# Down-projection sums issued at a wider spacing, and four raw buffers for the seven-product weight loads

## Chip, cores and metric

The kernel runs on one core of one Trainium2 chip. The metric is device time in microseconds for one execution of the whole program. Three runs of the kernel before are given, and one further execution was profiled.

## What is computed

Two layers (DEPTH = 2) of a hybrid encoder on a sequence of 512 tokens, width 1024, in float32. In short:

```python
for l in range(DEPTH):
    h = _rmsnorm(x, g_mix[l])
    proj = h @ w_in[l]            # gates (4 x 1024), conv input, q/k/v of three attentions
    y_a = _conformer_conv(...)    # branch 0
    y_b = _neighbourhood_attn(...)  # branch 1
    y_c = _dilated_attn(...)      # branch 2
    y_d = _window_gqa_sink(...)   # branch 3
    branch = jnp.einsum('bsnc,ncd->bsnd', ys, w_branch[l])
    gates = jax.nn.sigmoid(gate_pre + gate_b[l])
    x = x + jnp.sum(gates * branch, axis=2) @ w_out[l]
    x = x + _conv_ffn(_rmsnorm(x, g_ffn[l]), w_up[l], ffn_conv_w[l], ffn_conv_b[l], w_down[l])
```

`_conv_ffn` multiplies by `w_up` (1024 x 5632), applies a width-3 depthwise convolution, SwiGLU, and multiplies by `w_down` (2816 x 1024).

## The kernel before

All products are made from split operands: a float32 value is a rounded part `hi` plus a remainder `lo`, and each product is three matmuls (`hi*hi`, `hi*lo`, `lo*hi`). Activations lie with channels on the partitions (eight tiles of 128 x 512). Weights come in units of 128 x 1024 floats, 512 KB each. The method `weights` loads a unit: a DMA on SP's queue into a buffer `raw`, an ACT copy that rounds it to `hi` (line 252), and a DVE subtraction that gives `lo` (line 254). There are three `hi`, three `lo` and, for most units, two `raw` buffers (`w_raw`). A list `w_list` holds the units in order, each with a number in front. Units of the down-projection have the number 0, and for those a counter `w_fast` sends two of every four to two further buffers, `w_more`, that live in the pool of the feed-forward stage.

A layer runs in this order: token-major projections of q, k and v, the conformer branch's gated input (`glu`), then for the branches in the order 1, 2, 3, 0 the eight gate blocks of each branch (`gates`), the output projection, and the feed-forward stage. A block is 24 matmuls on one unit. In `gates`, each of the eight columns `d` ends with an elementwise chain: DVE multiplies the gate and the branch product into `t` (line 878), POOL adds it to the running sum `mx` (line 879; DVE does so for the last two columns of the last gate), and in the last gate ACT and DVE then split the sum into `mh` and `ml` (lines 883 and 884).

Beside the blocks run generators in `self.side`: attention, the convolution, and the transfers of sums described next. They advance by one step at each `tick`, which the code calls once in the middle of a block and once behind it. When the third gate is done, the line

```python
while self.side:
    self.tick()
```

runs what is left of them to the end, before the last gate (branch 0) is emitted.

The two large matrices of the feed-forward stage are multiplied in blocks of two by two with seven products instead of eight (a Strassen-Winograd form). That needs sums of weight blocks, S1 to S4, and these are formed by DMA: transfers from HBM to HBM on POOL's queue, some of which add into their destination. `quarter_sums` makes the sums for the up-projection (five groups of eight transfers, 512 KB each, line 1110), and `weight_sums` those for the down-projection (line 1133): four sums in three chunks, 1024, 1024 and 768 KB, 24 transfers. Each transfer is "paced": it may be issued only after the matmul that was emitted last. They are chained in one generator in `layer`:

```python
self.side.append(self.slowly(chain(self.quarter_sums(l), self.weight_sums(l))))
```

`slowly` waits 12 ticks, and then as many ticks after each transfer as the generator yields (one where it yields nothing). The order in `weight_sums` is: three copies into s3, three into s1, three additions into s3, three into s1, three copies of s3 into s2, three additions into s2, three copies of s2 into s4, three additions into s4. An operation on a chunk waits for the earlier one on which it depends.

In the feed-forward stage the up-projection runs over eleven groups of channels. Groups 2 to 6 use the seven-product form: `seven` takes one unit for each of the products, 24 matmuls of 256 columns on each (line 992). The units of A11, A22 and A12 come from the packed weights `W`, those of S1 to S4 from the sums (`qS` in the trace). The other groups are whole blocks. The down-projection follows (`down`), with units from `W` and from `sums`.

The order of instructions on each engine's queue is settled by a planner when the program is built, from priorities and its own times; weight loads are given a priority 3000 instructions ahead of their place.

Of the kernel before, what the change touches and what calls it, by code (L numbers as in the profile page):

```python
# [218 lines left out]
class Trunk:  # L219
# [7 lines left out]
    def weights(self, upto, ahead=3000, parts=1, queue=None):  # L227

        nc = self.nc
        while self.w_emitted < min(upto, len(self.w_list)):  # L230
            n, pieces = self.w_list[self.w_emitted]
            with self.tc.high_priority(offset=ahead):

                self.w_fast = (self.w_fast + 1) % 4 if n == 0 else 0
                if n == 0 and self.w_fast in (3, 0):
                    raw = self.fp.tile([P, 1024], F32, name="w_raw", tag="w_more", bufs=2)
                else:
                    raw = self.wpool.tile([P, 1024], F32, name="w_raw", tag="w_raw", bufs=2)
                hi = self.wpool.tile([P, 1024], F32R, name="w_hi", tag="w_hi", bufs=3)
                lo = self.wpool.tile([P, 1024], F32R, name="w_lo", tag="w_lo", bufs=3)  # L240
                src = pieces()
                n = sum(p.shape[1] for p in src)
                if len(src) == 1:
                    cut = [slice(i * n // parts, (i + 1) * n // parts) for i in range(parts)]
                    src = [src[0][:, s] for s in cut]
                c = 0
                for p in src:
                    (queue or nc.sync).dma_start(raw[:, c:c + p.shape[1]], p)
                    c += p.shape[1]
                for i in range(parts):  # L250
                    s = slice(i * n // parts, (i + 1) * n // parts)
                    w = nc.scalar.activation(hi[:, s], raw[:, s], AF.Copy)  # L252
                    self.first_hi = self.first_hi or w
                    nc.vector.tensor_tensor(lo[:, s], raw[:, s], hi[:, s].bitcast(F32), ALU.subtract)  # L254
            self.w_ready.append((hi, lo))
            self.w_emitted += 1
# [874 lines left out]
    def weight_sums(self, l):  # L1131

        add = lambda *a, **k: self.paced(self.nc.gpsimd.dma_start(*a, **k))
        items = []
        for c in range(0, NP2, CHUNK):
            n = min(CHUNK, NP2 - c)
            t = self.dram.tile([n * P, 4 * S], F32, name=f"sums{c}", tag=f"sums{c}", bufs=2)
            self.sums[l].append(t)
            src = self.all_quads[l][c * P:(c + n) * P]
            part = lambda x, i: x[:, i * S:(i + 1) * S]  # L1140
            items.append((part, t, src))
        s2, s1, s3, s4 = range(4)
        b11, b12, b21, b22 = range(4)
        for d, s in ((s3, b12), (s1, b11)):
            for part, t, src in items:
                add(part(t, d), part(src, s))
                yield 2
        for d, s in ((s3, b11), (s1, b21)):
            for part, t, src in items:
                add(part(t, d), part(src, s), accum_op=ALU.add)  # L1150
                yield 2
        for d, b, s in ((s2, s3, b21), (s4, s2, b22)):
            for part, t, src in items:
                add(part(t, d), part(t, b))
                yield 2
            for part, t, src in items:
                add(part(t, d), part(src, s), accum_op=ALU.add)
                yield 2

    def pair_tags(self, j):  # L1160

# [161 lines left out]
    def run(self):  # L1323
        nc, tc = self.nc, self.tc
        with ExitStack() as st:
            pool = lambda name, **k: st.enter_context(tc.tile_pool(name=name, bufs=1, **k))
            self.const = pool("const")
            self.xpool = pool("xparts")
            self.wpool = pool("weights")
            self.norm = pool("norm")  # L1330
            self.psum = pool("psum", space=PSUM)
            self.dram = pool("dram", space=bass.MemoryType.DRAM)
            self.w_list = []
            self.quads, self.sums, self.all_quads, self.quarters, self.qsums = [], [], [], [], []
            self.halves = {}
            for l in range(L):
                off, quads, quarters, ups, sums = 0, [], {}, {}, {}
                for kind, a, n in UNITS:
                    src = self.W[l, off:off + n * P].rearrange("(p c) -> p c", p=P)
                    off += n * P  # L1340
                    if kind == 'quad':
                        quads.append(src)
                    elif kind == 'quarter':
                        quarters[a] = src
                    elif kind == 'up':
                        ups[a] = src
                    else:
                        self.w_list.append((n, lambda src=src: [src]))
                for kind, a, b in UP_STEPS:
                    if kind == 'whole':  # L1350
                        self.w_list.append((1024, lambda src=ups[b * DFF + a * P]: [src]))
                    elif b[0] == 'A':
                        self.w_list.append((1024, lambda src=quarters[a, int(b[1]) - 1, int(b[2]) - 1]: [src]))
                    else:
                        self.w_list.append((1024, lambda s=sums, at=(a, b): [s[at]]))
                self.quarters.append(quarters)
                self.qsums.append(sums)
                self.quads.append(quads)
                self.sums.append([])
                self.all_quads.append(self.W[l, off - NP2 * 2048 * P:off].rearrange("(p c) -> p c", c=2048))  # L1360
                self.last_units(l)
            self.w_emitted = self.w_used = 0
            self.first_hi = None
            self.w_ready, self.w_fast = [], 0
            self.side, self.waiting, self.head = [], [], None

            self.cst = self.const.tile([P, NRES], F32, name="cst", tag="cst", bufs=1)
            self.ident = self.cst[:, C_ID:C_ID + P]
            self.prm = self.const.tile([P, NPAR], F32, name="prm", tag="prm", bufs=1)
            warm = self.const.tile([P, 1], F32, name="warm", tag="warm", bufs=1)  # L1370
            with tc.tile_pool(name="first", bufs=1, reuse_waits="tile") as first:

                z = first.tile([P, 256], F32R, name="zero", tag="zero", bufs=1)
                nc.vector.memset(z.bitcast(F32), 0.0)
                nc.vector.memset(warm, 0.0)
                ps = self.aux()
                for i in range(WARM):
                    nc.tensor.matmul(ps[:, :256], lhsT=z[:, :P], rhs=z, start=True, stop=True)
                self.sq_tag = "sq"
                self.start_norm('g_mix')  # L1380
                x0 = first.tile([P, KT + S], F32, name="x0", tag="x0", bufs=1)
                self.gains = lambda d: x0[:, d:d + 1]
                for d in range(KT):
                    if d == 0:
                        xn = x0[:, KT:]
                        for s in (slice(0, KT + 256), slice(KT + 256, KT + S)):
                            nc.sync.dma_start(x0[:, s], self.X0[:, s])
                    else:
                        xn = first.tile([P, S], F32, name="xn", tag="xn", bufs=7)
                        nc.sync.dma_start(xn, self.xT[d - 1])  # L1390
                    if d == 0:
                        self.weights(1, 0, 2, nc.scalar)
                        nc.scalar.activation(warm, warm, AF.Exp)
                    self.norm_tile(d, xn, first, d == 0)
                    if d in (1, 3):
                        self.weights(2 + d // 2, 0)
                    if d == 2:
                        nc.sync.dma_start(self.prm, self.PAR[0])
                nc.sync.dma_start(self.cst, self.CST[:, :NRES])
                self.finish_norm(7, 10)  # L1400
            self.xres = [self.X0[:, KT:]] + [self.xT[d] for d in range(KT - 1)]
            for l in range(L):
                self.layer(l)
# [124 lines left out]
```

## Time and profile before

| | |
|---|---|
| runs | 1597.1, 1598.54, 1599.13 us |
| median | 1598.54 us |
| profiled execution | 1600.03 us, of which its span 1598.3 us |
| mean granted TensorE clock | 0.991 |
| busy in the span | PE 97%, DVE 78%, ACT 56%, POOL 13% |
| DMA queue of SP | 212.10 MB, 41.6% of 16 engines |
| DMA queue of POOL | 92.81 MB, 26.0% of 16 engines |

PE is TensorE's matmuls, PEld its weight loads, DVE VectorE, ACT ScalarE, POOL GpSimd, SP the engine that issues most DMAs. A "q" behind an engine's name is its queue (SPq). Shares are of the span. A row of the timeline gives the start in us, the duration, the engine, the line of the kernel, the operation and its tiles, and in brackets how long the engine had been idle and what ended that; "x2" marks neighbours that are merged. Rows of DMA issues show the issue and not the transfer. Row labels such as `sums<-W` read "written from".

### The profile page before, as it was taken

The numbers are of one execution on the slowest core, as the hardware profiler recorded it, in microseconds if no ns is written. First come the engines' busy times: TensorE is split into PE (matmuls) and PEld (weight loads), VectorE is DVE, ScalarE is ACT, GpSimd is POOL, SyncE is SP. The second block draws the span as 40 slices with busy tenths as digits, with TensorE's granted clock in tenths as the row PEclk, the third lists the DMA queues.
The fourth block names the chain that finished last, engine by engine and source line by source line (L and its number), as shares of the span: only waits on it lengthen the run. The fifth ranks groups of instructions, "written<-read, shape, count | busy, mean of one in ns | idle before, by whom it ended". The sixth has DMA issues, their size and how long they took to land.

```text
span 1598.3 us, 21942 instructions
## 1 busy us (share of the span) xinstructions
PE 1547.3 (97%) x7842; PEld 1312.7 (82%) x7842; DVE 1252.9 (78%) x2114; ACT 895.3 (56%) x1504; POOL 204.3 (13%) x308
## 2 busy tenths in 40 slices
PE   9999999996999999999999999999969999899999
PEld 8888888884889988888888878888858898888887
DVE  6699988752689989895676989887446888899964
ACT  6778777332456655563557677763234555554642
POOL 0044112332100000000002231132221000000000
PEclk9999999998999999999999999999989999999999
DMA  7789786999654543366567978769986466633565
GB/s 234 225 226 244 190 204 191 214 230 231 202 177 132 175 160 128 93 202 203 178 195 224 242 208 198 197 186 234 245 204 222 158 166 187 185 122 104 174 215 172
DMA packets 124797, 306.84 MB, mean 192 GB/s; under 512 B 28176, under 2 KB 30096, under 8 KB 124688
## 3 DMA queue, kind: packets, MB, share of 16 engines
q1 hardware_dynamic: 93712, 212.10, 41.6%
q0 software_dynamic: 30688, 92.81, 26.0%
q8 instruction: 62, 1.02, 0.3%
q10 hardware_dynamic: 288, 0.52, 0.1%
q14 instruction: 47, 0.39, 0.1%
HBM read 287.56 MB, written 100.67 MB: 243 GB/s over the span
## 4 chain that ended last, share of the span: by engine, by line
PE 73%; DMA 10%; DVE 9%; ACT 5%; issue 2%; POOL 1%; ACTq 0%; DVEq 0%; POOLq 0%
PE mm L273 14%; PE mm L275 14%; PE mm L274 14%; PE aux L992 4%; DVE w_lo L254 3%; DMA w_raw<-W 3%; DMA w_raw<-qS 3%; DMA sums<-W 3%; PE aux L1224 2%; PE aux L1223 2%; PE aux L1225 2%; ACT w_hi L252 2%; PE mm L1224 2%; PE mm L1223 2%; PE mm L1225 2%
## 5 line engine op out<-in xcount | busy, mean ns | idle before, releaser
L252 ACT ACTIVATE w_hi<-w_raw 128x1024 fp32r<-128x1024 f32 (+1 forms) x335 | 350.6, 1047 | 360.9 <-PE mm L274 127.9
L254 DVE TENSOR_TENSOR w_lo<-w_raw,w_hi 128x1024 fp32r<-128x1024 f32 (+1 forms) x335 | 406.3, 1215 | 110.3 <-ACT w_hi L252 108.6
L273 PE MATMUL mm<-xh,w_hi 128*128 128x512 f32 x960 | 377.0, 393 | 28.1 <-DVE t L849 27.1
L275 PE MATMUL mm<-xh,w_lo 128*128 128x512 f32 x960 | 375.8, 391 | 0.0
L274 PE MATMUL mm<-xl,w_hi 128*128 128x512 f32 x960 | 375.4, 391 | 0.0
L273 PEld LDWEIGHTS mm<-xh,w_hi 128*128 128x128 f32 x960 | 181.2, 189 | 65.9 <-ACT w_hi L252 27.9
L275 PEld LDWEIGHTS mm<-xh,w_lo 128*128 128x128 f32 x960 | 180.8, 188 | 39.5 <-DVE w_lo L254 1.4
L274 PEld LDWEIGHTS mm<-xl,w_hi 128*128 128x128 f32 x960 | 181.3, 189 | 36.2
L992 PE MATMUL aux<-form,w_hi 128*128 128x256 f32 x640 | 117.2, 284 | 1.3 <-ACT w_hi L252 1.1
L992 PEld LDWEIGHTS aux<-form,w_hi 128*128 128x128 f32 x640 | 99.8, 192 | 2.3 <-ACT w_hi L252 2.1
L440 DVE SCALAR_TENSOR_TENSOR cv<-cv,prm 128x512 f32<-128x512 f32 x120 | 94.0, 783 | 0.7
L992 PE MATMUL aux<-form,w_lo 128*128 128x256 f32 x320 | 91.0, 285 | 2.5 <-DVE w_lo L254 2.5
L1033 ACT ACTIVATE cy<-U,prm 128x512 f32<-128x512 f32 x88 | 69.9, 806 | 26.2 <-DVE U L1017 14.3
L879 POOL TENSOR_TENSOR mx<-mx,t 128x512 f32<-128x512 f32 x44 | 63.1, 1440 | 133.6 <-DVE t L878 133.5
L502 PE MATMUL mm<-w_hi,xh 128*128 128x512 f32 x192 | 76.4, 398 | 0.4 <-DVE V L630 0.4
L503 PE MATMUL mm<-w_lo,xh 128*128 128x512 f32 x192 | 75.0, 390 | 0.0
L504 PE MATMUL mm<-w_hi,xl 128*128 128x512 f32 x192 | 74.8, 390 | 0.0
L1110 POOL DMA_DIRECT2D qS<-W x60 | 43.7, 728 | 218.0 <-PE aux L780 107.2
L767 ACT ACTIVATE e<-e,rl 128x256 f32<-128x256 f32 (+2 forms) x96 | 57.4, 598 | 22.0 <-DVE rl L766 21.5
L1034 DVE SCALAR_TENSOR_TENSOR cy<-U,prm,cy 128x512 f32<-128x512 f32 x88 | 64.7, 745 | 6.2 <-ACT cy L1033 6.2
L849 DVE TENSOR_TENSOR t<-mm,RB 128x512 f32<-128x512 f32 x64 | 43.8, 685 | 29.3 <-PE mm L275 29.2
L1035 DVE SCALAR_TENSOR_TENSOR cy<-U,prm,cy 128x512 f32<-128x512 f32 x88 | 64.8, 745 | 0.8
(339 smaller groups left out, 3193.0 us busy)
## 6 DMA issues: line engine op xcount, KB each, us to landing
w_raw<-W SPq DMA_DIRECT2D x213, 512.0 KB, 3.7
qS<-W POOLq DMA_DIRECT2D x60, 512.0 KB, 6.4
sums<-W POOLq DMA_DIRECT2D x24, 1024.0 KB, 13.7
w_raw<-qS SPq DMA_DIRECT2D x40, 512.0 KB, 3.5
w_raw<-W SPq DMA_DIRECT2D x66, 256.0 KB, 3.9
w_raw<-sums SPq DMA_DIRECT2D x44, 256.0 KB, 4.0
w_raw<-sums SPq DMA_DIRECT2D x22, 512.0 KB, 4.6
qS<-qS POOLq DMA_DIRECT2D x20, 512.0 KB, 4.8
```

The lines of the kernel that those rows point to most:

```text
L252: w = nc.scalar.activation(hi[:, s], raw[:, s], AF.Copy)
L254: nc.vector.tensor_tensor(lo[:, s], raw[:, s], hi[:, s].bitcast(F32), ALU.subtract)
L273: mm(ps, lhsT=wh, rhs=xh, start=start, stop=False)
L274: mm(ps, lhsT=wh, rhs=xl, start=False, stop=False)
L275: self.last_mm = mm(ps, lhsT=wl, rhs=xh, start=False, stop=stop)
L440: self.after_mm(v.scalar_tensor_tensor(acc, u[:, t:t + S], w(t), acc, ALU.mult, ALU.add))
L502: mm(pss[b], lhsT=self.Xh[k][:, t], rhs=hi[:, s], start=k == 0, stop=False)
L503: mm(pss[b], lhsT=self.Xh[k][:, t], rhs=lo[:, s], start=False, stop=False)
L504: self.last_mm = mm(pss[b], lhsT=self.Xl[k][:, t], rhs=hi[:, s], start=False, stop=k == KT - 1)
L992: self.last_mm = nc.tensor.matmul(o, lhsT=w[:, s], rhs=x, start=start and not (e or j or i), stop=j == 3 and i == 2, skip_group_check=True)
L1033: nc.scalar.activation(y, u[:, 1:513], AF.Identity, scale=w(1), bias=self.par('ffn_conv_b', c))
L1035: v.scalar_tensor_tensor(y, u[:, 2:514], w(2), y, ALU.mult, ALU.add)
```

## The change

There are two edits. In `weight_sums`, each `yield 2` becomes `yield 4`: a down sum for every four ticks (half blocks) instead of two. In the list of units, those of the seven-product groups get the number 1 instead of 1024, and `weights` lets units with that number take `w_more` and `w_raw` by turns, so that they go through four raw buffers instead of two. The count by which the down-projection's units choose their buffers is not altered, since whole units stand before them and set `w_fast` to 0.

```diff
-                self.w_fast = (self.w_fast + 1) % 4 if n == 0 else 0
-                if n == 0 and self.w_fast in (3, 0):
+                self.w_fast = (self.w_fast + 1) % 4 if n < 2 else 0
+                if n == 0 and self.w_fast in (3, 0) or n == 1 and self.w_fast % 2 == 1:
                     raw = self.fp.tile([P, 1024], F32, name="w_raw", tag="w_more", bufs=2)
                 else:
                     raw = self.wpool.tile([P, 1024], F32, name="w_raw", tag="w_raw", bufs=2)
...
         for d, s in ((s3, b12), (s1, b11)):
             for part, t, src in items:
                 add(part(t, d), part(src, s))
-                yield 2
+                yield 4
...
# the same in the other three loops of weight_sums
...
                     elif b[0] == 'A':
-                        self.w_list.append((1024, lambda src=quarters[a, int(b[1]) - 1, int(b[2]) - 1]: [src]))
+                        self.w_list.append((1, lambda src=quarters[a, int(b[1]) - 1, int(b[2]) - 1]: [src]))
                     else:
-                        self.w_list.append((1024, lambda s=sums, at=(a, b): [s[at]]))
+                        self.w_list.append((1, lambda s=sums, at=(a, b): [s[at]]))
```

More of the change, by code (lines that the diff above doesn't have):

```diff
@@ L1150, in weight_sums @@
                 add(part(t, d), part(src, s), accum_op=ALU.add)
-                yield 2
+                yield 4
         for d, b, s in ((s2, s3, b21), (s4, s2, b22)):
@@ L1154, in weight_sums @@
                 add(part(t, d), part(t, b))
-                yield 2
+                yield 4
             for part, t, src in items:
                 add(part(t, d), part(src, s), accum_op=ALU.add)
-                yield 2
+                yield 4
     def pair_tags(self, j):
```

## The prediction

> **What bounds the kernel now.** I read the head of the page first, then the waits, then the timeline of POOL around the one place where PE stands still, then busy time by stretches.
>
> ```profile
> span 1598.3 us, 21942 instructions
> PE 1547.3 (97%) x7842; PEld 1312.7 (82%) x7842; DVE 1252.9 (78%) x2114; ACT 895.3 (56%) x1504; POOL 204.3 (13%) x308
> ```
>
> PE is busy 1547.3 of 1598.3 us: TensorE is the bound, and only 51.0 us of the span are not matmul. Whatever the change does to the time, it does by shortening or lengthening those 51.0 us. The waits say where the largest pieces lie.
>
> ```profile
> ACT mh L883 <- POOL mx L879: 67.4, 10, 23.7
> DVE ml L884 <- ACT mh L883: 60.1, 10, 23.2
> PE mm L273 <- DVE t L849: 27.1, 2, 14.9
> ```
>
> Columns: who waited for whom, total us, times, longest. PE waits twice (once in each layer) for the DVE product `t` of line 849, 27.1 us in all. The two rows above it say why DVE is late: `ml` waits for ACT's `mh`, which waits up to 23.7 us for POOL's addition `mx` (line 879). So in each layer POOL holds up ACT, DVE and then PE. What POOL does at that time, in layer 0 (start, us, engine, line, operation, and in brackets its idle time and what ended it):
>
> ```profile
> 227.76 0.66 POOL L1133 DMA_DIRECT2D sums<-W  x1 [2.71 <-PE aux L780]
> 236.24 0.65 POOL L1133 DMA_DIRECT2D sums<-W  x1 [7.82 <-PE aux L780]
> ...
> 322.38 0.67 POOL L1133 DMA_DIRECT2D sums<-sums  x1 [5.86 <-PE aux L478]
> ...
> 333.24 0.64 POOL L1133 DMA_DIRECT2D sums<-sums  x1
> ...
> 340.16 0.59 POOL L1133 DMA_DIRECT2D sums<-sums  x1
> 340.77 1.68 POOL L879 TENSOR_TENSOR mx<-mx,t 128x512 f32<-128x512 f32 x1
> 342.39 2.12 POOL L1133 DMA_DIRECT2D sums<-W  x2
> 347.02 0.95 POOL L1133 DMA_DIRECT2D sums<-W  x1 [2.51 <-DMA sums<-sums]
> 358.24 0.66 POOL L1133 DMA_DIRECT2D sums<-sums  x1 [10.26 <-DMA sums<-W]
> 365.40 0.65 POOL L1133 DMA_DIRECT2D sums<-sums  x1 [6.51 <-DMA sums<-W]
> 369.72 0.59 POOL L1133 DMA_DIRECT2D sums<-sums  x1 [3.67 <-DMA sums<-W]
> 373.03 1.04 POOL L1133 DMA_DIRECT2D sums<-W  x1 [2.72 <-DMA sums<-sums]
> 376.27 1.04 POOL L1133 DMA_DIRECT2D sums<-W  x1 [2.20 <-DMA sums<-sums]
> 378.41 0.95 POOL L1133 DMA_DIRECT2D sums<-W  x1 [1.09 <-DMA sums<-sums]
> 379.02 1.63 POOL L879 TENSOR_TENSOR mx<-mx,t 128x512 f32<-128x512 f32 x1
> ```
>
> There are 24 down-sum transfers in a layer. Fourteen are issued one by one from 227.76 to 333.24. From 340.16 on, ten are issued in a row, each as soon as the transfer that it reads from has landed, and the first `mx` addition of the last gate stands behind all ten, at 379.02. In between PE uses up its four banks and stops. This is the place the first edit touches.
>
> **Why ten, and how many after it.** The two generators that transfer sums advance by one step at each tick, and a tick comes twice in a block. From the place where they are started to the end of the third gate the code ticks 80 times: 8 in each of the three `token_major` projections, 8 in `glu`, 16 in each of three `gates`. Before: 12 ticks of waiting, 40 quarter sums at one each, leaves 28 ticks; at two each that is 14 down sums. The rest, 10, is issued by `while self.side: self.tick()`, a loop with no matmul in it, so that pacing by the last matmul no longer holds anything apart. The rows agree: the 15th issue is the one at 340.16. After: 28 ticks at four each are 7 down sums, and 17 go through the loop. The wider spacing thus applies to seven transfers and takes the spacing from seven more. In order these seven are numbers 8 to 14: two additions into s3, three into s1, and two copies s3 to s2, that is 5 accumulating transfers and 2 copies.
>
> **Price of a transfer.** Windows of layer 0 (busy us of each engine with counts, granted clock, DMA share, GB/s):
>
> ```profile
> 227.00:282.00 55.00, 55.00 (x270) 46.20 (x269) 47.28 (x97) 40.89 (x103) 15.30 (x14) 1.00 0.63 191
> 282.00:310.00 28.00, 28.00 (x126) 23.12 (x126) 20.02 (x27) 8.55 (x13) 8.04 (x8) 1.00 1.04 218
> 310.00:343.00 33.00, 33.00 (x155) 27.41 (x154) 24.79 (x46) 14.03 (x18) 11.39 (x11) 1.00 0.92 235
> 343.00:368.00 25.00, 24.83 (x110) 20.24 (x108) 5.56 (x6) 3.90 (x5) 3.77 (x5) 1.00 1.06 239
> 368.00:383.00 15.00, 0.22 (x1) 0.25 (x2) 1.66 (x3) 1.91 (x3) 4.92 (x5) 0.64 1.05 242
> 460.00:495.00 35.00, 35.00 (x156) 29.00 (x155) 35.00 (x56) 20.65 (x26) 0.00 (x0) 1.00 0.34 112
> ```
>
> The last row has whole up-projection blocks and no sums: weight loads alone take 0.34 of the DMA engines while PE runs. From 227 to 282 six copies are issued; they account for (0.63 - 0.34) x 55 = 16 us, or 2.7 us each. From 282 to 343 six additions and a little over two copies: (1.04 - 0.34) x 28 + (0.92 - 0.34) x 33 = 38.7 us; less 2.3 x 2.7, by six, 5.4 us for an addition (it reads its destination too). From 343 to 383 the share is 1.06 and 1.05: in the loop the DMA engines are full, and the issues come at the rate at which transfers finish. Check on the loop as it is: 7 transfers must land before the 24th can be issued, three additions and four copies, 16.2 + 10.8 = 27.0 us, and loads for the 27 us for which PE still runs, 9.2 us: 36.2. Layer 0 took 378.41 - 340.16 = 38.3 us, and layer 1:
>
> ```profile
> 1133.29 0.59 POOL L1133 DMA_DIRECT2D sums<-sums  x1
> ...
> 1169.02 0.94 POOL L1133 DMA_DIRECT2D sums<-W  x1 [0.72 <-DMA sums<-sums]
> ```
>
> 35.7 us, on average 37.0, or 1.02 times the price.
>
> **First edit, the sum.** Removed from the gates: seven transfers a layer. It saves nothing there, since PE is busy 55.00 of 55, 28.00 of 28 and 33.00 of 33 us in those stretches; DMA time that was hidden by matmuls is what is given up. Added to the loop: 5 x 5.4 + 2 x 2.7 = 32.4 us, by 1.02, 33 us a layer. None of it is hidden: PE stops after the same blocks as now, since it is DVE that stands at `ml` and the banks that run out, and no weight load is added while it stands. So PE's standstill grows from about 15 to about 48 us in layer 0 and from 12 to 45 in layer 1: +66 us. Behind the first `mx` on POOL stand the next additions, and behind them the residual loads of the up-projection; they shift as a whole. The first load that reads the sums is issued ahead, on SP:
>
> ```profile
> 454.35 0.86 SPq L248 DMA_DIRECT2D w_raw<-sums  x2
> ```
>
> that is 75 us after the last issue of sums, and both shift alike, so their landing keeps its cover. Bounds: the seven move 4,608 + 2,048 KB, 6.82 MB; at the 242 GB/s of the row 368 to 383 that is 28 us a layer (+56). If each of the seven costs what the loop's seven cost on average, 38.3/7 and 35.7/7 us, it is +74. If all the loop's time but the copies belonged to its three additions, (38.3 - 10.8)/3 = 9.2 us each, it would be 5 x 9.2 + 5.4 = 51 a layer, +103. I take 33, since the prices by share reproduce the loop to 2%; the issue instructions are 0.6 to 1.1 us each and vanish in the waits.
>
> **Second edit.** No instruction is added or taken away: the same loads go into four buffers in turn. What limits the seven-product stage now (layer 1, chain and windows):
>
> ```profile
> 1338.66 1.14 DVE w_lo L254
> 1339.82 4.35 DMA w_raw<-qS
> 1344.28 1.07 ACT w_hi L252
> 1345.37 1.24 DVE w_lo L254
> 500.00:540.00 40.00, 40.00 (x335) 40.00 (x334) 37.27 (x52) 25.19 (x33) 0.00 (x0) 1.00 0.54 175
> 540.00:600.00 60.00, 56.59 (x452) 54.92 (x451) 53.72 (x70) 36.13 (x47) 0.00 (x0) 1.00 0.52 166
> 1290.00:1410.00 120.00, 109.33 (x845) 104.38 (x844) 105.72 (x139) 67.96 (x90) 0.00 (x0) 1.00 0.63 181
> ```
>
> A load may start only when the DVE subtraction has freed its buffer; load, ACT copy and subtraction then take 1346.6 - 1339.8 = 6.8 us, for two buffers 3.4 us a unit, while a unit of 24 matmuls of 256 columns takes 40/335 x 24 = 2.9 us of PE. With four buffers that ring is 1.7 us a unit and no longer binds. PE's idle time there is 3.4 + 10.7 = 14.1 us, the most there is to gain. What comes next is DVE: it is busy 53.72 of 60 and 105.72 of 120 us, and where PE had no gap (500 to 540) it reached 37.27 of 40, 93%. At 93% the two stretches take 57.8 and 113.7 us: 2.2 + 6.3, I take 8 us. Ends: 0 (DVE is late anyway) and 14.
>
> **Sum.** The profiled execution took 1600.0 us, a span of 1598.3 and 1.7 around it; the median of the runs is 1598.5, 1.5 lower, and I add to that. 1598.5 + 66 - 8 = 1656.5, so 1656 us.
>
> **Rivals.** (A) The order on POOL's queue is settled when the program is built, by a planner that goes by its own times. With a longer loop it may put the first `mx` of the last gate ahead of the last few issues. It interleaves like that in the gates (340.77 stands between two issues), but in the loop it left all ten ahead, seven of them waiting. Each column let through gives PE about one interval of the later additions,
>
> ```profile
> 384.51 1.28 POOL L879 TENSOR_TENSOR mx<-mx,t 128x512 f32<-128x512 f32 x1 [3.86 <-DVE t L878]
> 389.64 1.28 POOL L879 TENSOR_TENSOR mx<-mx,t 128x512 f32<-128x512 f32 x1 [3.86 <-DVE t L878]
> ```
>
> 5.1 us: one a layer, 1656 - 10 = 1646. (B) Transfers that follow each other without a pause run faster than these prices: at a copy's 2.7 us for all seven, 18.9 a layer, 1598.5 + 38 - 8 = 1628. Against it: the share is already 1.05 in the loop. The Trainium skill, "DMA: Bandwidth & Descriptors", section Bandwidth, has transfers gain with size, up to 425 GB/s for 16 MB; by that the extra 6.82 MB would take an estimated 16 us a layer and the time would be 1623. That section measures loads from HBM into SBUF; the rows here, HBM to HBM with additions, show 242 GB/s at a full share, so the trace does not agree. (C) Additions are dearer, 9.2 us, because full engines slow them: 1598.5 + 103 - 8 = 1693. For it: the issue at 358.24 waited 10.26 us for the first; against it, the next two follow after 7.2 and 4.3. (D) The other side: the planner puts the last gate's `mx` additions ahead of every issue that has to wait. Then the 27.1 us of standstill go as well, 1598.5 - 27 - 8 = 1563. It decides from the point at which at least seven of the 17 stand behind the first `mx`, since then no more stand ahead than the ten now. Against it: the ten rows above.
>
> **How the numbers follow.** My forecast, 17 transfers ahead of the first `mx` at these prices, has 0.66, and its own range is 1640 to 1674 (from 28 us a layer with the full 14 gained, to +74 with nothing gained, rounded). A 0.15, B 0.05, C 0.09, D 0.05. The range 1632 to 1680 takes in A with cheap transfers and half of what lies between my forecast and C; outside are B, D and most of C, under 0.2. A difference of 0.2%, 3.2 us, is about what a measurement can tell from none; only D can be faster (0.04) or the same (0.01), the rest, 0.95, is slower.
>
> **What would show it.** Right: seven down-sum issues from about 228 to 325 us, then 17 in a row from about 340; the first `mx` after them near 412 instead of 379; PE still from about 367 to 415 with a DMA share near 1; the wait of PE on DVE's `t` near 93 us instead of 27.1; the same in layer 1. In 1290 to 1410 (shifted) PE idle of 4 to 6 us instead of 10.7, with ACT's wait for loads from the quarter sums mostly gone and DVE above 0.9. Wrong: `mx` rows of the last gate between the issues (A, D), issue spacings under 3 us (B) or above 8 for additions (C), or PE idle unchanged in the seven-product stage.

## The result, and the profile after

The changed kernel takes 1638.9 us (median, 1637.9 to 1641.2) against 1598.8 us before on the same chip: a ratio of 1.0254, 95% interval 1.0236 to 1.0272. It is 40.1 us slower. The prediction said 1656, with 1632 to 1680 as its range.

The head of the page and the waits (who waited for whom, total us, times, longest us) after the change:

```profile
span 1637.4 us, 21918 instructions
PE 1541.0 (94%) x7842; PEld 1311.0 (80%) x7842; DVE 1251.0 (76%) x2114; ACT 895.8 (55%) x1504; POOL 205.4 (13%) x308
...
PE mm L273 <- DVE t L849: 89.5, 2, 45.1
ACT mh L883 <- POOL mx L879: 130.9, 10, 55.7
DVE ml L884 <- ACT mh L883: 123.8, 11, 55.2
```

The three waits of before are the same three, with the same count on PE: two standstills, now 89.5 us together instead of 27.1. Below is what POOL did in layer 0, as a timeline:

```profile
337.36 1.02 POOL L1133 DMA_DIRECT2D sums<-W  x1
338.04 1.65 POOL L879 TENSOR_TENSOR mx<-mx,t 128x512 f32<-128x512 f32 x1
339.27 3.41 POOL L1133 DMA_DIRECT2D sums<-W  x3
351.42 0.95 POOL L1133 DMA_DIRECT2D sums<-W  x1 [8.74 <-issue]
356.62 1.32 POOL L1133 DMA_DIRECT2D sums<-sums  x2 [4.25 <-issue]
365.55 0.59 POOL L1133 DMA_DIRECT2D sums<-sums  x1 [7.61 <-issue]
377.85 1.05 POOL L1133 DMA_DIRECT2D sums<-W  x1 [11.70 <-DMA sums<-sums]
...
408.15 0.95 POOL L1133 DMA_DIRECT2D sums<-W  x1 [1.25 <-DMA sums<-sums]
408.76 1.62 POOL L879 TENSOR_TENSOR mx<-mx,t 128x512 f32<-128x512 f32 x1
```

Seven issues stand in the gates (not shown, 227.35 to 322.08); the eighth is the one at 337.36, the first of the 17 that follow each other to 408.15. The first addition of the last gate is at 408.76, where the prediction had 412. The loop took 70.8 us here and 70.1 in layer 1, against 38.3 and 35.7 before. PE stands still from 367 until this:

```profile
412.52 0.76 PE L273 MATMUL mm<-xh,w_hi 128*128 128x512 f32 x1 [45.10 <-DVE t L849]
```

The seven-product stage went the other way. Windows over it, the changed kernel first and the one before below it (busy us with counts, granted clock, DMA share, GB/s):

```profile
525.00:623.30 98.30, 98.30 (x819) 98.18 (x819) 93.35 (x122) 64.71 (x85) 0.00 (x0) 1.00 0.55 178
1340.00:1438.00 98.00, 98.00 (x816) 97.88 (x815) 94.07 (x122) 63.61 (x82) 0.00 (x0) 1.00 0.74 205
```

```profile
495.00:598.00 103.00, 99.59 (x817) 98.18 (x816) 93.75 (x122) 63.88 (x83) 0.00 (x0) 1.00 0.51 163
1286.00:1399.00 113.00, 102.33 (x817) 98.88 (x816) 99.16 (x130) 64.12 (x84) 0.00 (x0) 1.00 0.64 183
```

The same number of matmuls, 816 or a few more, takes 98.0 us after and 103.0 and 113.0 before. After the change a matmul follows each 0.12 us with no gap.

Stage times from the starts of matmuls in the two traces, in us:

| from, to | before | after | difference |
|---|---|---|---|
| last gate, branch matmuls, layer 0 | 54.23 | 85.03 | +30.8 |
| the same, layer 1 | 52.06 | 84.83 | +32.8 |
| 34 seven-product units, layer 0 | 102.99 | 97.79 | -5.2 |
| the same to the next stage, layer 1 | 203.08 | 187.88 | -15.2 |
| end of layer 0's down-projection to the first branch of layer 1 | 160.61 | 156.95 | -3.7 |
| everything else | | | -0.4 |

(The fourth row runs on to the start of the down-projection.) The sum is 39.1 us, the difference of the two spans.

### The profile page after: what moved, and what is told of

The parts are those of the page before. It is cut to its first block, busy times and chain, and to the rows that moved or that the text cites. A ratio compares the mean times of both kernels' runs of the same rounds, so it can differ in the third digit from the quotient of the medians.

```text
span 1637.4 us, 21918 instructions
## 1 busy us (share of the span) xinstructions
PE 1541.0 (94%) x7842; PEld 1311.0 (80%) x7842; DVE 1251.0 (76%) x2114; ACT 895.8 (55%) x1504; POOL 205.4 (13%) x308
## 4 chain that ended last, share of the span: by engine, by line
PE 83%; DMA 6%; DVE 4%; ACT 3%; issue 3%; POOL 2%; SPq 0%; POOLq 0%; ACTq 0%; DVEq 0%
PE mm L273 15%; PE mm L274 15%; PE mm L275 15%; PE aux L992 11%; DMA sums<-sums 4%; PE aux L1225 2%; PE aux L1223 2%; PE aux L1224 2%; PE mm L502 2%; PE mm L504 2%; PE mm L503 2%; PE mm L1224 2%; PE mm L1225 2%; PE mm L1223 2%; PE mm L992 2%
## 5 line engine op out<-in xcount | busy, mean ns | idle before, releaser
L273 PE MATMUL mm<-xh,w_hi 128*128 128x512 f32 x960 | 377.3, 393 | 89.5 <-DVE t L849 89.5
L884 DVE SCALAR_TENSOR_TENSOR ml<-mx,mh 128x512 fp32r<-128x512 f32 x16 | 11.0, 690 | 124.0 <-ACT mh L883 123.8
L883 ACT ACTIVATE mh<-mx 128x512 fp32r<-128x512 f32 x16 | 10.0, 627 | 135.4 <-POOL mx L879 130.9
```

The lines of the kernel that those rows point to most:

```text
L273: mm(ps, lhsT=wh, rhs=xh, start=start, stop=False)
```

## Experiments

Each of the first three kernels below differs from one of the two in one thing. Theory Q, mine: POOL works its queue in order, the issues of sums in the loop wait there for earlier transfers, and the additions that the last gate needs stand behind them; the number of transfers in the loop sets the time. Rival D: it is the DMA traffic itself that costs, wherever the additions stand.

**The two edits apart.** First edit alone: the four `yield 4` in the kernel before. Second alone: `yield 2` put back in the changed kernel.

> The first edit alone (a down sum for every four ticks, two raw buffers as before). Theory Q: the time of the loop that issues what is left of the sums sets how long PE stands still, and the second edit acts elsewhere. Then this run has the standstills of the changed kernel, 45.1 + 44.4 = 89.5 us against 27.1, and the seven-product stages of before: 1598.8 + 62 + 1 = 1662 us. Rival R: a part of the gain in the seven-product stages comes from the first edit (sums out of the way earlier or later, loads that come otherwise): then the units of layer 1 take clearly less than the 112.8 us of before, and the time is 1640 to 1655. The start of layer 1 up to the first sum took 228.0 us before and 224.4 after; 224.4 here would put that to the first edit.

> The second edit alone (four raw buffers, a sum for every two ticks). Theory Q: the standstills are those of before, 27.1 us together, and the 34 units between the first and the last but one of a layer take 97.8 us in each layer (no gap at all) instead of 103.0 and 112.8: 1598.8 - 20.2 = 1578 us, or 1575 if the 3.6 us at the start of layer 1 go with this edit. My prediction's value for this edit, 8 us with DVE as the next limit, gives 1591; the 14.1 us of PE idle that the profile counts give 1585.

Measured: the first edit alone 1661.1 us (ratio to before 1.0408, 1.0372 to 1.0444), the second alone 1576.0 us (0.9869, 0.9842 to 0.9896). The stages are as independent as theory Q has them. With the first edit alone the 34 units take 103.7 and 113.8 us as before, and PE stands still 86.3 us. With the second alone they take 97.8 us twice, and PE stands still 23.6 us. The waits of each (first edit, then second):

```profile
PE mm L273 <- DVE t L849: 86.3, 2, 44.0
```

```profile
PE mm L273 <- DVE t L849: 23.6, 2, 14.1
```

Rival R falls. The start of layer 1 took 228.1 us with the first alone and 227.7 with the second alone, against 224.4 with both, so the 3.7 us of the table belong to neither edit alone.

**The additions off POOL's queue.** In the changed kernel:

```diff
-        (v if n == ORDER[3] and d >= 6 else nc.gpsimd).tensor_tensor(m, m, t, ALU.add)
+        (v if n == ORDER[3] else nc.gpsimd).tensor_tensor(m, m, t, ALU.add)
```

> The changed kernel, with all eight mx additions of the last gate on DVE (before: the first six on POOL). The 17 transfers stay where they are on POOL's queue, but nothing that PE needs stands behind them. Theory Q (the queue): the standstill goes, PE waits for DVE's t under 10 us in all, six DVE additions of 0.7 us a layer lie beside matmuls: 1638.9 - 89.5 + 0 to 8 = 1550 to 1558 us. Rival D (full DMA engines): it is the transfers themselves that hold up the last gate by delaying weight loads, wherever the additions stand; then the 70 us of 17 transfers at a share near 1 still cost half or more of the standstill, 1590 us or more, with PE waiting for ACT's w_hi, and that for loads.

Measured: 1575.0 us (0.9868, 0.984 to 0.9895), midway between the two. The last gate's branch matmuls take 37.40 us in both layers, and the wait of PE for DVE's `t` is gone from the list: the standstill was POOL's queue, as theory Q says. But 26 us of the 89.5 come back behind it (30 by the stage times: the two last gates became 95 us shorter, since behind a standstill about ten matmuls also start some 0.43 us apart, at a granted clock of 0.50 from 412.5 to 415.5 in the changed kernel, and later ones 0.23). From the end of the output projection to the first seven-product matmul it takes 54.9 and 55.9 us instead of 44.65, and the output projection 47.7 and 46.7 instead of 42.84. Windows of this kernel, and a stretch of its chain of waits (start, us, what):

```profile
370.00:400.00 30.00, 27.32 (x120) 22.08 (x119) 18.47 (x25) 10.23 (x14) 3.70 (x4) 1.00 1.05 276
400.00:415.00 15.00, 15.00 (x61) 12.22 (x60) 6.36 (x8) 4.87 (x7) 2.28 (x3) 0.89 1.04 327
415.00:460.00 45.00, 39.62 (x155) 30.01 (x154) 24.43 (x36) 19.16 (x27) 6.53 (x14) 0.92 1.01 303
```

```profile
376.61 8.08 DMA w_raw<-W
384.80 1.07 ACT w_hi L252
385.89 1.24 DVE w_lo L254
387.14 8.47 DMA w_raw<-W
...
427.58 11.96 DMA w_raw<-W
```

With PE at work the full DMA engines (share 1.01 to 1.05) carry loads and sums together, and a weight load takes 8 to 12 us; it took 3.8 in the median of the whole execution of the changed kernel. The residual's stores `res` and loads `xf`, on which the way to the seven-product stage depends, slow down as well: 6.3 us against 2.8 and 8.9 against 3.9, medians of the two executions. So the cost that rival D names is there, but it is a third of the standstill and not the half or more that rival D had. In the changed kernel it did not show: there the output projection and the way behind it take the 42.84 and 44.65 us of before, and PE was standing while the sums went through.

**Additions or copies.** The changed kernel with `accum_op=ALU.add` left out everywhere in `weight_sums`, so that the sums are not formed; only its times are used.

> The changed kernel with every additive transfer of the down sums turned into a plain copy of the same size and place in the queue (so the sums are not formed). In the loop 14 transfers must land before the last issue. By the prices of the prediction (5.4 us an addition, 2.7 a copy, loads of 0.34 for 27 us) it goes from 70.5 to 14 x 2.7 + 9.2 = 47 us, the standstills from 89.5 to about 43, the time from 1638.9 to about 1592. Rival: additions and copies cost the same in a full queue, because bytes or issues limit it: the loop stays at 65 to 71 us and the time above 1625.

Measured: 1604.0 us, one run. The loop takes 50.6 and 51.1 us instead of 70.8 and 70.1, the standstills 49.6:

```profile
338.82 0.63 POOL L1133 DMA_DIRECT2D sums<-W  x1
...
389.43 0.59 POOL L1133 DMA_DIRECT2D sums<-W  x1 [1.23 <-DMA sums<-sums]
390.03 1.27 POOL L879 TENSOR_TENSOR mx<-mx,t 128x512 f32<-128x512 f32 x1
```

Of the 14 transfers that must land before the last issue eight were additions; turning them into copies saved 20.2 us in layer 0 and 19.0 in layer 1, 2.5 and 2.4 us each, near the 2.7 of the prices (5.4 less 2.7). The rival, equal cost, falls. The loop takes 50.6 us and not 47 although a copy costs what the prices say, since the DMA engines are not full in it:

```profile
339.00:390.00 51.00, 29.88 (x132) 24.40 (x130) 7.31 (x8) 5.10 (x6) 11.82 (x18) 0.82 0.94 320
```

0.94 x 50.6 is 47.6 us of their time, less 9.2 for loads, by 14, 2.7 us a copy. That makes the standstills 6.6 us longer than the 43 expected. The rest of the 12 us between 1592 and 1604 lies outside the loop: 2.5 us at the start of layer 1 and 1.4 before the first gate, against the changed kernel.

**Carrying the sums on.** Two kernels in which the loop stops when only the sums are left, one at four ticks and one at two (the second edit in both):

```diff
-                self.side.append(self.slowly(chain(self.quarter_sums(l), self.weight_sums(l))))
+                slow = self.slowly(chain(self.quarter_sums(l), self.weight_sums(l)))
+                self.side.append(slow)
...
-                while self.side:
+                while any(g is not slow for g in self.side):
```

> The changed kernel, but the loop behind the third gate no longer runs the sums to the end: it stops when only the generator of the sums is left, and the remaining 17 transfers go on at one for every four ticks through the last gate and the up-projection. Theory Q: the loop is the cause of the standstill, both by the queue and by the full DMA engines, and with the transfers apart neither remains: 1638.9 - 89.5 = 1549 us, PE waiting for DVE's t under 5 us. Rival D: the sums cost their DMA time wherever they run; most of them now fall into the seven-product stage, whose loads already take a DMA share of 0.55 to 0.74, and 13 transfers of about 5 us each in it bring back 10 us or more of waits for loads: 1560 us or more.

> The second edit alone (one transfer for every two ticks) with the same carrying on past the third gate: ten transfers are left, and eight of them fall into the last gate. Theory Q: the 24.4 us of standstill of the second edit alone go: 1576 - 24 = 1552 us. Against the kernel that carries on at four ticks, the difference shows what the wider spacing is worth when the loop is out of the way: if transfers two ticks apart hold up the mx additions of the last gate (issues that wait for the transfer before them, a DMA share of 1.04 as from 282 to 310), 5 to 15 us, 1557 to 1567; if not, the two are equal within 3 us.

Measured: 1583.8 us (0.9926, 0.991 to 0.9943) at four ticks, 1571.8 us (0.9848, 0.9833 to 0.9863) at two. The last gate takes 37.40 us in both, with no loop no standstill. Both miss the 1549 and 1552 of theory Q, for two reasons. At four ticks the sums are still running in the seven-product stage, whose 34 units take 112.5 us in layer 1 instead of 97.8, at a DMA share of 0.96 there (second row; the first is layer 0):

```profile
489.00:588.00 99.00, 98.29 (x817) 98.02 (x816) 92.82 (x121) 64.59 (x84) 7.99 (x9) 1.00 0.90 263
1269.00:1381.00 112.00, 99.86 (x813) 98.85 (x812) 93.71 (x121) 62.51 (x81) 7.98 (x9) 0.97 0.96 254
```

That is rival D's cost, 14.7 us. In layer 0 nine sums run beside the stage as well and cost 1.0 us (98.8 us). Without sums the share is 0.55 there and 0.74 in layer 1 (the windows after the change), so that layer 1 has less room; that this is the whole reason is not shown. And in both kernels the way from the output projection to the first seven-product matmul takes 55.7 to 58.3 us. POOL in the kernel with two ticks:

```profile
437.26 1.05 POOL L1133 DMA_DIRECT2D sums<-W  x1 [46.52 <-DVE xl L336]
...
438.05 4.25 POOL L943 DMA_DIRECT2D xf<-res  x7
451.07 0.54 POOL L943 DMA_DIRECT2D xf<-res  x1 [8.77 <-DMA sums<-W]
```

One sum stands 46.5 us on POOL: by the code it is paced by a matmul in the first block behind the output projection, and the profile names DVE's `xl`, which that block reads, as what ended the wait. The residual loads `xf` that the seven-product forms are made of stand behind it; seven go out at once at 438. With no sum in front (the second edit alone) they go out one by one from 421. Two ticks came out 12 us faster than four, where the expectation had them equal or two ticks slower: the seven-product stage, which that expectation did not price, costs 15.7 us more at four ticks. The same queue, a second time, with loads behind the waiting issue instead of additions. To test that, the loads went to SP:

```diff
-                nc.gpsimd.dma_start(x[:, e * S:(e + 1) * S], self.xres[2 * j + e])
+                nc.sync.dma_start(x[:, e * S:(e + 1) * S], self.xres[2 * j + e])
```

> The kernel that carries the sums on past the third gate at two ticks, with one difference: the eight residual loads xf, with which the seven-product forms are made, go out on SP's queue and not on POOL's. In that kernel the last gate had no standstill (37.4 us), but from the end of the output projection to the first seven-product matmul it took 55.9 and 58.3 us instead of 44.65, with seven xf loads issued at once at 438 behind a sum that had waited 46.5 us. Theory Q: that loss is POOL's queue once more; with the loads on SP it takes 44.65 us again and the time is 1571.8 - 24.9 = 1547 to 1550 us. Rival: it is the sums' DMA traffic; then the loads land no earlier, and the time stays at 1565 us or more. A third way: the loads stand behind waiting weight loads on SP instead and come late there, 1555 to 1565.

Measured: 1562.5 us (0.9788, 0.9767 to 0.9808), the third way. The stretch falls to 52.9 and 53.4 us, not to 44.65. The first loads still go out only at 437.71, now behind the weight loads on SP:

```profile
437.19 0.42 SPq L248 DMA_DIRECT2D w_raw<-W  x1
437.71 1.03 SPq L943 DMA_DIRECT2D xf<-res  x2
441.96 0.33 SPq L248 DMA_DIRECT2D w_raw<-W  x1
442.33 2.44 SPq L943 DMA_DIRECT2D xf<-res  x5
```

So moving them took 8.0 us off the two stretches together and put them behind another queue. That POOL's queue alone made the whole loss is not shown; that the forms wait for loads that leave late is (waits of the kernel with two ticks, 434 to 492, and the same kernel with the loads on SP, 425 to 485):

```profile
ACT xf L950 <- DMA xf<-res: 10.8, 1, 10.8
```

```profile
ACT xf L950 <- DMA xf<-res: 13.3, 6, 4.6
```

**Fewer in the loop, additions on DVE.** With 26 us left to the full engines, a loop of ten instead of 17 should lose less.

> All additions of the last gate on DVE, as in the run before, but with the spacing of two ticks, so ten transfers in the loop. With 17 in the loop 1575.0 us were left where 1549 would be with no standstill: 26 us for loads that took 8 us instead of 3.7 beside full DMA engines. If that loss goes with the time for which the engines are full (38 of 71 us), it is 14 us here: 1563 us. If it is set by something else (the residual loads and the first up-projection units behind the loop), it stays near 26: 1575 us. If it goes away, 1550 us.

Measured: 1550.9 us (0.9718, 0.9703 to 0.9732). The last gate takes 37.40 us, the output projection 44.4 and 45.9, and the way to the seven-product stage is back at 44.65. The loss is 4.6 us, not the 14 of a loss in proportion. With ten in the loop the last issue stands before the output projection, which begins at 390.6; with 17 it was at 418.96, and the output projection began at 391.9:

```profile
377.42 0.95 POOL L1133 DMA_DIRECT2D sums<-W  x1 [0.64 <-DMA sums<-sums]
```

So most of the stretch in which loads were late at 17 is spared. This version beats both kernels.

**The other spacings.**

> Four raw buffers, and a sum for every tick: 24 transfers in the 28 ticks left before the third gate ends, none in the loop. By the prices, from the first sum to the end of the third gate (113 us): 12 x 5.4 + 12 x 2.7 = 97 us of sums and 0.34 x 113 = 38 us of loads, 135 us, 22 more than there are. Theory Q: with no loop there is no standstill at the last gate, and the full engines cost at most the excess: 1549 to 1572 us. Rival: transfers one tick apart have to wait for each other on POOL ahead of the mx additions of the second and third gate, whose t buffers are two, so PE stands in those gates instead: 1580 us or more.

> The changed kernel with one transfer for every three ticks: ten transfers in the gates, 14 in the loop (two additions into s1 and two copies more than with a spacing of two, two additions fewer... in all: 11 and 12 as additions, 13 and 14 as copies are what is added to the ten). Theory Q, by the prices of the prediction: 2 x 5.4 + 2 x 2.7 = 16.2, by 1.02 16.5 us a layer over the spacing of two, which stood at 24.4 us with four raw buffers: 24.4 + 33 = 57 us of standstill and 1576.0 + 33 = 1609 us. If the standstill does not go with the transfers in the loop but jumps at some spacing, it is near 1576 or near 1639.

One per tick: 1575.1 us (0.9864, 0.9844 to 0.9884), 3 us above what theory Q allowed and below its rival. The last gate has no standstill, but the third gate, from its first to its last branch matmul, takes 49.8 and 52.3 us instead of 39.3. The mechanism is the rival's, only smaller: in the third gate of layer 0 DVE's `t` waits for POOL's additions, which stand behind issues that wait for transfers (waits from 297 to 370, and two rows of POOL's timeline). Of PE's own idle time 7.3 us wait for a DVE product of the convolution, `cv`, which stands behind such a `t` in DVE's queue, and 2.3 for `t` of line 849:

```profile
POOL sums L1133 <- DMA sums<-sums: 17.2, 2, 14.2
DVE t L878 <- POOL mx L879: 16.7, 3, 10.3
PE aux L478 <- DVE cv L469: 7.3, 1, 7.3
```

```profile
304.32 1.05 POOL L1133 DMA_DIRECT2D sums<-W  x1 [14.15 <-DMA sums<-sums]
...
310.85 1.64 POOL L879 TENSOR_TENSOR mx<-mx,t 128x512 f32<-128x512 f32 x1
```

One per three ticks: 1611.0 us (1.0091, 1.0073 to 1.0108), 2 us from what the prices give, with PE standing still

```profile
PE mm L273 <- DVE t L849: 58.0, 2, 30.2
```

58.0 us where 57 was expected. (Two expectations give 24.4 us for the second edit alone; its waits add up to 23.6.) With four raw buffers the standstill is thus 23.6, 58.0 and 89.5 us for 10, 14 and 17 transfers in the loop: it goes with what the loop must wait for, and does not jump.

## Why the prediction was right, and where it was off

The count was right: 7 issues in the gates, 17 in the loop, in both layers. The wait was right: the additions stayed behind all 17 (rivals A and D did not happen), and PE stopped at 367 and went on at 412.5, where the prediction had 367 and 415. The waits of PE for `t` came to 89.5 us, where it had about 93.

The number was nearer to the edge than the mechanism deserved. 1638.9 us lies inside 1632 to 1680 but below the 1640 to 1674 that the forecast gave itself (its upper end, +74, makes 1672.5 and not 1674); the room below 1640 was left for rival A, which did not happen. That the result fell into it is luck. Of the 18 us between the forecast +58 and the measured +40, about 12 are the second edit, 4 the start of layer 1 and 2 the last gates, which grew by 63.6 and not 66.

The price of the loop was right to a few per cent: +33 us a layer forecast, +32.5 and +34.4 measured in the loop, 66.9 together where the sum had 66. PE's standstill grew by 62.4: the loop also starts earlier, 110.0 us after the first sum instead of 112.4 in layer 0 and 109.0 instead of 111.2 in layer 1. Rival B (transfers faster without a pause) falls, and so does the time of 16 us a layer that the prediction works out for it from the 425 GB/s of the Trainium skill ("DMA: Bandwidth & Descriptors", section Bandwidth; a figure for 16 MB, where the transfers here are 1 MB or less): the extra 6.82 MB took 32.5 and 34.4 us. Rival C (9.2 us an addition, 51 us more a layer) falls with a loop of 70.8 us and not 89.

That taking seven transfers out of the gates saves nothing was right: between the first branch matmuls of the second, third and last gate the traces differ by 0.03 us or less, before and after.

The term that was mis-sized is the second edit: 8 us forecast, with 14 as the most there is to gain; it measured 20.4 us by the stage times, and alone it makes the kernel 20.6 us faster. Two steps of it failed. The first: "PE's idle time there is 3.4 + 10.7 = 14.1 us, the most there is to gain". Waiting was counted as busy: 99.59 and 102.33 us for 817 matmuls before, where 816 take 98.00 after. A matmul's record is 0.28 us long here (median) while the next one starts after 0.12 us, so that the first 0.16 us of every gap look busy. The starts before show 16 gaps in layer 0 and 35 in layer 1, 20.4 us in all, of which 6.4 us stood inside the busy time. For the same reason "only 51.0 us of the span are not matmul" was no bound on what can be gained: the same 7842 matmuls are busy for 1547.3 us before and 1541.0 after. The spacing of matmul starts would have shown it: 40/335 us each, a number that stood in the prediction, makes 97.5 us of 817, against 103 and 113. The second: "What comes next is DVE", with 93% as its ceiling. After the change DVE is busy 93.35 of 98.30 and 94.07 of 98.00 us, 95 and 96%, and PE has no gap. A utilization reached with no gap on PE is what DVE had to do, not what it could.

The term that is missing is the start of layer 1, 3.7 us of the 40. In the twelve traces that stretch takes between 156.4 us (carrying on at four ticks) and 160.7 us (first edit alone). One weight load in it accounts for the difference. From issue to landing it took 16.8 us before and 13.1 after (rows of the list of DMA issues, before first; the last number is the time to landing):

```profile
w_raw<-W SPq DMA_DIRECT2D x1, 512.0 KB, 16.8
```

```profile
w_raw<-W SPq DMA_DIRECT2D x1, 512.0 KB, 13.1
```

The stretch less this load is 143.8 to 144.0 us in all twelve traces, and the DMA share around it is 1.06 in both. Why the load is longer in some is open. Neither edit alone shortens it (16.8 and 16.5 us), and no run here was made to tell chance from cause.

## What to carry to other kernels

A pace that is counted in steps of other work must be checked against the number of steps there are: what does not fit is issued in one heap, and a wider spacing then makes the heap larger. Keep instructions on which the critical engine depends off an in-order queue on which DMA issues wait for other DMAs, and keep the heap small too, because what no longer waits in the queue waits for the full DMA engines. Judge what a stall on TensorE costs by the spacing of matmul starts in a stretch without gaps, not by the idle time that the profile counts.

## What the runs showed of the hardware

HBM to HBM transfers of about 1 MB that add into their destination cost 2.4 to 2.5 us more than plain copies of the same size in a loop that fills the DMA engines or nearly so (70.8 against 50.6 us, and 70.1 against 51.1, with eight of them changed). Beside full engines, SP's 512 KB weight loads were not starved but slowed to two to three times their time, 8.1, 8.5 and 12.0 us (additions on DVE) against 3.8.
